# Two transformer blocks on one core: the last gate stage and the final norm with tokens on the rows

## The chip, the core and the metric

The kernel runs on one core of a Trainium2 chip. The core has five engines that work side by side, each through its own instructions in order: TensorE (PE, matrix products), VectorE (DVE), ScalarE (ACT), GpSimd (POOL) and SyncE (SP), which here only starts transfers. What one engine needs of another it waits for at a semaphore. The metric is the time of one execution on the device in microseconds (us), the median of several runs.

## The reference, cut to what matters

The whole program is two blocks of a transformer over 256 tokens of 1024 features, in float32: a feed-forward and attention block, then a block with a convolution, a forgetting attention ("fox") and two more feed-forwards. The change touches its end:

```python
def second_block(x, p, ...):
    for i in range(2):
        ...                                   # convolution (i = 0) or fox attention (i = 1)
        hn = rmsnorm_2(h, ffn_norm[i])
        h = h + jnp.square(jax.nn.relu(hn @ ffn_w1[i])) @ ffn_w2[i]
        gate = jax.nn.sigmoid(rmsnorm_2(h, ple_norm[i]) @ ple_w_gate[i])
        h = h + gate * (p[i] @ ple_w_proj[i])
    return rmsnorm_2(h, final_norm)
```

`p[i]` is 256 tokens by 256 features, `ple_w_gate[i]` is 1024 by 1024, `ple_w_proj[i]` 256 by 1024. `rmsnorm` divides a token's features by the root of their mean square and multiplies by a gain for each feature.

## The kernel before

**Layout.** Activations lie with the features on the 128 rows (partitions) and the 256 tokens along a row: eight tiles `self.x[0..7]` of 128x256. A product `dense(name, c0, X)` (lines 252 to 254) loads a 128x128 block of weights as the stationary operand and streams the 256 tokens of one X tile through it. Precision is kept by splitting both operands in a high and a low part, so that each block takes three products (weights high by X high, weights high by X low, weights low by X high). ScalarE makes the high part of a chunk of weights (L231) and VectorE the low part (L235); a chunk is eight blocks, four chunks are held converted at a time.

**The other layout**, `v_steps` (L1014 to L1016), makes the tokens the rows: 128 tokens of X are the stationary operand and 512 columns of weights stream through it. Before the change only the values of attention are made so.

**The end of fox.** The list FOX orders work that fills TensorE between the steps of the sixteen heads. Its last entry, `e1`, is `values(1)`: eight groups of `ple_value` (p times `ple_w_proj`, each group six products of 256 columns into one bank, then a scaling by 0.5 on ScalarE, L1101). The order of TensorE is written out by hand there; behind it come the products of the output weights `wo`, which a scheduler places. A head is: scores (L1036), softmax, a transpose on TensorE (L1075), a copy out by ScalarE (L1077), and the product with the values (L1471).

**Banks.** The accumulators of TensorE are eight banks in four kinds of two: `mm`, `s`, `pt`, `at`. `bank("mm")` walks through the kinds listed for the stage in CYCLE (in the heads only `mm`, in `wo` and in the feed-forward `mm`, `at`, `s`, in the last stage `mm` and `at`). A bank is written again only after its readers are done.

**The last stage, `ple(1, ...)` and `run`.** Column sums of squares on TensorE (L376) give the norm; VectorE (L390), GpSimd (L385, the power -0.5) and two products (L400) spread it over the rows as R. Then eight groups of 24 products each: VectorE multiplies by R (L1129), ScalarE takes tanh (L1130), VectorE forms (tanh + 1) times the value (L1132) and adds it to x (L1086). ScalarE squares the new x (L365) and multiplies it by the gain of the final norm (L1592), VectorE adds up the squares (L368), and TensorE transposes the gained tile for the two halves of the tokens (L1595). After the last group come the column sums of the squares, L390, L385, four scalings of 128x512 (L1603 on VectorE, L1605 on ScalarE) and four transfers of 256 KB to the output (L1606, two from SP's queue and two from ScalarE's).

Of the kernel before, what the change touches and what calls it, by code (L numbers as in the profile page):

```python
# [16 lines left out]
P = 128  # L17
# [99 lines left out]
class Kern:  # L117
# [887 lines left out]
    def v_steps(self, name, X, half, bks):  # L1005

        nc = self.nc
        bks.extend(self.bank() for _ in range(2))
        for k in range(KD):
            wk = self.weight(name, k, half * 512, 512)  # L1010
            for t in range(2):
                s = slice(t * P, (t + 1) * P)
                xh, xl = X[k][0][:, s], X[k][1][:, s]
                nc.tensor.matmul(bks[t], xh, wk[0], start=(k == 0), stop=False)  # L1014
                nc.tensor.matmul(bks[t], xl, wk[0], start=False, stop=False)
                nc.tensor.matmul(bks[t], xh, wk[1], start=False, stop=(k == KD - 1))  # L1016
                if (k, t) != (KD - 1, 1):
                    yield

# [103 lines left out]
    def ple(self, i, X, R, pv, after):  # L1123
        nc = self.nc
        self.stage = f"ple{i}"
        for n in range(KD):
# [6 lines left out]
            self.residual(t, n, after)  # L1133

# [203 lines left out]
    def fox(self, Xk, rc, R, after):  # L1338
# [143 lines left out]
        def values(i):  # L1482
            X = [self.split(t) for t in loads]
            for n in range(KD):
                pv.append(self.ple_value(i, n, X))
# [44 lines left out]
    def run(self, out):  # L1530
# [53 lines left out]
        _, R = self.stats(st["acc"])  # L1584
        f = {"acc": None}
        self.cycle = CYCLE["end"]
        tb = [[self.bank(tag) for _ in range(2)] for tag in ("s", "pt")]

        def after(n, x):
            f["acc"] = self.square_into(f["acc"], x, n == KD - 1)  # L1590
            xg = self.t("t")
            nc.scalar.mul(xg, x, self.col("final2", n))  # L1592
            for t in range(2):
                o = tb[t][n // 4][:, (n % 4) * P : (n % 4 + 1) * P]
                nc.tensor.transpose(o, xg[:, t * P : (t + 1) * P], self.ident)  # L1595

        self.ple(1, st["X"][0], R, pv, after)
        r = self.rsqrt(self.mean_eps(self.col_sums(f["acc"], "mm"), 2, D), 2)
        for t in range(2):
            for i in range(2):  # L1600
                o = self.p([P, 512], "o", 4)
                if i:
                    nc.vector.tensor_scalar(o, tb[t][i], r[:, t : t + 1], None, op0=ALU.mult)  # L1603
                else:
                    nc.scalar.mul(o, tb[t][i], r[:, t : t + 1])  # L1605
# [131 lines left out]
```

## Time and profile before

| | us |
|---|---|
| median of 3 runs (1384.69 to 1385.52) | 1385.49 |
| the profiled execution | 1383.3 |
| its span, first to last instruction | 1381.5 |
| last gate stage, first product to start of the last (1345.63 to 1371.00) | 25.4 |
| from the start of the last product to the end of the span | 10.5 |

The profiled execution lasts 1.8 us beyond its span and is 2.2 us under the median of the runs. TensorE is busy for 98% of the span; its weight loads (PEld) overlap its products.

### The profile page before, as it was taken

To read this page: it belongs to the slowest core of one execution; us is meant where nothing else is said; L and a number is where in the kernel's file an instruction comes from. 1 tells how busy PE (TensorE), PEld (TensorE's weight loads), DVE (VectorE), ACT (ScalarE), POOL (GpSimd) and SP (SyncE) were. 2 spreads that over 40 slices of the span, in tenths; PEclk is the share of its full clock that TensorE was granted. 3 is DMA by queue.
4 is the path that set the end of the run, shared out by engine and by line. 5 is a ranking of instruction groups with operands and counts; after the bars stand their busy time and mean duration, and the time that the engine had idled before them with its cause. 6 is when DMAs were issued, how large, how long until landed. Compare 5 with 4: busy or idle time off the path is not lost.

```text
span 1381.5 us, 28847 instructions
## 1 busy us (share of the span) xinstructions
PE 1360.4 (98%) x11191; PEld 1325.2 (96%) x11191; DVE 1031.1 (75%) x2306; ACT 828.2 (60%) x1875; POOL 42.4 (3%) x89
## 2 busy tenths in 40 slices
PE   9999999999999999999999999999999999999997
PEld 8999998899988999999999999999998999999997
DVE  7777658798886778876679797765578987776555
ACT  6555445678787555555555586654457786665444
POOL 0000000000000000000000000000001310000000
PEclk9999999999999999999999999999999999999999
DMA  7555556633332645555566145555554334555550
GB/s 271 186 184 184 184 182 231 226 138 108 123 105 80 199 161 193 194 182 184 183 228 227 56 153 187 187 182 182 185 178 169 133 119 152 192 189 183 183 183 35
DMA packets 65385, 234.87 MB, mean 170 GB/s; under 512 B 7552, under 2 KB 8224, under 8 KB 65248
## 3 DMA queue, kind: packets, MB, share of 16 engines
q1 hardware_dynamic: 63792, 231.42, 48.6%
q8 instruction: 88, 1.44, 0.4%
q10 hardware_dynamic: 1296, 1.35, 0.3%
q0 software_dynamic: 160, 0.26, 0.1%
q14 instruction: 49, 0.40, 0.1%
HBM read 231.95 MB, written 1.05 MB: 169 GB/s over the span
## 4 chain that ended last, share of the span: by engine, by line
PE 93%; issue 2%; DVE 2%; ACT 1%; DMA 1%; SPq 0%; POOLq 0%; DVEq 0%; POOL 0%; ACTq 0%
PE mm L252 12%; PE mm L253 12%; PE mm L254 12%; PE at L252 8%; PE at L253 8%; PE at L254 8%; PE s L252 7%; PE s L254 7%; PE s L253 7%; PE pt L1190 3%; PE pt L1075 1%; PE s L1036 1%; PE at L819 1%; DVE lo L235 1%; PE pt L376 1%
## 5 line engine op out<-in xcount | busy, mean ns | idle before, releaser
L231 ACT ACTIVATE hi<-raw 128x512 fp32r<-128x512 f32 (+1 forms) x760 | 473.5, 666 | 410.8 <-issue 227.1
L235 DVE TENSOR_TENSOR lo<-raw,hi 128x512 fp32r<-128x512 f32 (+1 forms) x760 | 537.5, 742 | 166.2 <-ACT hi L231 164.2
L252 PE MATMUL mm<-a,hi 128*128 128x256 f32 x1046 | 304.6, 291 | 1.4 <-ACT hi L231 1.4
L253 PE MATMUL mm<-a,hi 128*128 128x256 f32 x1046 | 296.2, 283 | 0.0
L254 PE MATMUL mm<-a,lo 128*128 128x256 f32 x1046 | 295.8, 283 | 0.0
L252 PEld LDWEIGHTS mm<-a,hi 128*128 128x128 f32 x1046 | 200.4, 192 | 4.5 <-issue 2.3
L253 PEld LDWEIGHTS mm<-a,hi 128*128 128x128 f32 x1046 | 200.2, 191 | 0.0
L254 PEld LDWEIGHTS mm<-a,lo 128*128 128x128 f32 x1046 | 199.9, 191 | 0.2 <-DVE lo L235 0.2
L252 PE MATMUL at<-a,hi 128*128 128x256 f32 x622 | 177.4, 286 | 1.8 <-ACT hi L231 1.6
L254 PE MATMUL at<-a,lo 128*128 128x256 f32 x622 | 177.2, 285 | 0.2 <-DVE lo L235 0.2
L253 PE MATMUL at<-a,hi 128*128 128x256 f32 x622 | 177.3, 285 | 0.0
L252 PE MATMUL s<-a,hi 128*128 128x256 f32 x516 | 147.1, 285 | 1.0 <-ACT a L1272 1.0
L254 PE MATMUL s<-a,lo 128*128 128x256 f32 x516 | 146.8, 285 | 0.2 <-DVE lo L235 0.2
L253 PE MATMUL s<-a,hi 128*128 128x256 f32 x516 | 146.7, 284 | 0.0
L252 PEld LDWEIGHTS at<-a,hi 128*128 128x128 f32 x622 | 118.8, 191 | 2.7 <-ACT hi L231 1.8
L254 PEld LDWEIGHTS at<-a,lo 128*128 128x128 f32 x622 | 119.2, 192 | 1.4 <-DVE lo L235 0.4
L253 PEld LDWEIGHTS at<-a,hi 128*128 128x128 f32 x622 | 118.9, 191 | 0.7 <-DVE a L346 0.5
L252 PEld LDWEIGHTS s<-a,hi 128*128 128x128 f32 x516 | 99.5, 193 | 1.3 <-ACT a L1272 1.2
L254 PEld LDWEIGHTS s<-a,lo 128*128 128x128 f32 x516 | 99.4, 193 | 0.4 <-DVE lo L235 0.4
L253 PEld LDWEIGHTS s<-a,hi 128*128 128x128 f32 x516 | 99.5, 193 | 0.0
L253 PE MATMUL at<-H,hi 128*128 128x256 f32 x324 | 91.7, 283 | 0.0
L252 PE MATMUL at<-H,hi 128*128 128x256 f32 x324 | 91.7, 283 | 0.0
(411 smaller groups left out, 2795.9 us busy)
## 6 DMA issues: line engine op xcount, KB each, us to landing
raw<-in_wts SPq DMA_DIRECT2D x424, 512.0 KB, 3.4
cw<-in_dwp SPq DMA_DIRECT2D x9, 704.0 KB, 4.5
x<-in_xT SPq DMA_DIRECT2D x4, 256.0 KB, 5.6
raw<-in_wts SPq DMA_DIRECT2D x2, 256.0 KB, 3.7
e<-in_pT ACTq DMA_DIRECT2D x4, 128.0 KB, 4.2
out_dram<-o ACTq DMA_DIRECT2D x2, 256.0 KB, 3.0
out_dram<-o SPq DMA_DIRECT2D x2, 256.0 KB, 3.1
cst<-in_cst SPq DMA_DIRECT2D x1, 416.0 KB, 8.1
```

Source lines behind the costliest of these rows:

```text
L231: nc.scalar.activation(hi[:, s], raw[:, s], AF.Copy)
L235: nc.vector.tensor_tensor(lo[:, s], raw[:, s], hi[:, s].bitcast(F32), op=ALU.subtract)
L252: nc.tensor.matmul(out, sh, mh, start=(first and i == 0), stop=False)
L253: nc.tensor.matmul(out, sh, ml, start=False, stop=False)
L254: nc.tensor.matmul(out, sl, mh, start=False, stop=(last and i == n - 1))
L376: self.ins = self.nc.tensor.matmul(b[:, t : t + 1], p[:, t * P : (t + 1) * P], self.ones[:, 0:1], start=(i == 0), stop=(i == len(parts) - 1),)
L819: nc.tensor.matmul(o[e * HD : (e + 1) * HD, kt * P :], V[:, kt, 2 * i + g], pt[i][:, k], start=False, stop=(i == 1 and kt == 1),)
L1036: nc.tensor.matmul(o, q[:, t * P : n], k[:, :n], start=(t == 1 and i == 0), stop=False)
L1075: nc.tensor.transpose(tb[:, o * P : (o + 1) * P], a, self.ident)
L1190: nc.tensor.matmul(o, w[:, d], x[:, g, 16 - d : 16 + P - d], start=(d == 0), stop=(d == LAGS - 1))
```

## The change

The last gate stage and the values that it needs are made with the tokens on the rows, so that the output needs no transpose after the last product.

- `values(1)` goes through `v_steps`, now for any number of X tiles: two halves of 512 columns, each of two tiles of X and two halves of the tokens, 12 products of 512 columns for a half, into two banks at once; each bank is then scaled in two pieces of 128x256 (L1575 in the new file).
- The new function `last_ple` takes the place of `ple(1, ...)`. The gains of the final norm are fetched once, the same row for all 128 partitions (a transfer on ScalarE's queue). The old x is transposed by 16 products (L1158) as soon as it is there and added to the value (L1163). The first half of the columns is made for both halves of the tokens; the second half first for tokens 0 to 127, 512 columns wide, then for tokens 128 to 255 in two pieces of 256 columns.
- `quarter`: tanh out of the bank with the norm as a scale for each row (L1170), times the value (L1171), added to x (L1173), squared with the sum along the row given out by ScalarE itself (L1175), times the gain (L1182; not for the last quarter).
- `store(t)`: norm from the four sums (L1186, L385), scaling of four quarters, shared by VectorE and ScalarE (L1189, L1190, L1193, L1194, L1196), and two transfers of 256 KB. `store(0)` stands between the products of the two halves of the tokens.
- Gone: the products that spread R (L400, two instructions), the products with R on VectorE, the final column sums on TensorE (four instructions), the gain on ScalarE.

```diff
+    def rows3(self, o, x, t, w, first, last):
+        nc = self.nc
+        s = slice(t * P, (t + 1) * P)
+        xh, xl = x[0][:, s], x[1][:, s]
+        nc.tensor.matmul(o, xh, w[0], start=first, stop=False)
+        nc.tensor.matmul(o, xl, w[0], start=False, stop=False)
+        nc.tensor.matmul(o, xh, w[1], start=False, stop=last)
...
+    def last_ple(self, X, acc, pv, out):
...
+        nc.scalar.dma_start(gains, bass.AP(tensor=src.tensor, offset=src.offset, ap=[[0, P], [1, D]]))
+        rh = self.w([P, 2], "r1", 1)
+        nc.vector.tensor_scalar(rh, self.rsqrt(self.mean_eps(self.col_sums(acc), 2, D), 2), 0.5, None, op0=ALU.mult)
...
+                for n in range(4):
+                    nc.tensor.transpose(
+                        tb[:, n * P : (n + 1) * P], self.x[4 * half + n][:, t * P : (t + 1) * P], self.ident
+                    )
...
+        def quarter(t, q, o):
+            g = self.t("u")
+            nc.scalar.activation(g, o, AF.Tanh, scale=rh[:, t : t + 1])
+            nc.vector.tensor_tensor(g, g, pv[4 * t + q], op=ALU.mult)
+            v = x[t][q // 2][:, q % 2 * T : q % 2 * T + T]
+            nc.vector.tensor_tensor(v, v, g, op=ALU.add)
+            sq = self.t("sq")
+            nc.scalar.activation(sq, v, AF.Square, accum_out=ss[:, t, q : q + 1])
...
+            if q < 3:
+                nc.vector.tensor_tensor(v, v, gains[:, q * T : (q + 1) * T], op=ALU.mult)
+        def store(t):
+            v = self.w([P, 1], "rs_1", 2)
+            nc.vector.tensor_scalar(v, ss[:, t, 3:4], 1.0 / D, pre[:, t : t + 1], op0=ALU.mult, op1=ALU.add)
+            r = self.rsqrt(v, 1)
+            a, b = x[t]
+            nc.vector.scalar_tensor_tensor(b[:, T:], b[:, T:], r, gains[:, 3 * T :], op0=ALU.mult, op1=ALU.mult)
+            nc.scalar.mul(b[:, :T], b[:, :T], r)
+            nc.sync.dma_start(out[t * P : (t + 1) * P, 512:], b)
+            if t:
+                nc.vector.tensor_scalar(a[:, :T], a[:, :T], r, None, op0=ALU.mult)
+                nc.scalar.mul(a[:, T:], a[:, T:], r)
+            else:
+                nc.scalar.mul(a, a, r)
+            nc.scalar.dma_start(out[t * P : (t + 1) * P, :512], a)
...
             X = [self.split(t) for t in loads]
-            for n in range(KD):
-                pv.append(self.ple_value(i, n, X))
+            pv.extend([None] * KD)
+            for half in range(2):
+                yield from self.v_steps(f"pp_{i}", X, half, bks := [])
+                for t in range(2):
+                    for j in range(2):
+                        v = pv[4 * t + 2 * half + j] = self.a()
+                        nc.scalar.mul(v, bks[t][:, j * T : (j + 1) * T], 0.5)
                 yield
```

A scheduler orders the instructions, so the change moves some that the diff does not name. On TensorE at the end of fox (`pt`: transpose of the last head, `at_...<-PTh`: its product with the values, `y`: the heads' results that `wo` takes; `mm`, `s`, `at_...<-y`: products of three column groups of `wo`), before:

```order
L254 MATMUL s_15805<-y_15708,lo_15809 128x256
L1075 MATMUL pt_15736<-cst,P_15683 128x128 x3
L1471 MATMUL at_15742<-PTh_15716,VS_14224 64x256
L1471 MATMUL at_15742<-PTh_15740,VS_14224 64x256
L1471 MATMUL at_15742<-PTh_15716,VS_14224 64x128
L1471 MATMUL at_15742<-PTh_15740,VS_14224 64x128
L252 MATMUL mm_15691<-y_15747,hi_15694 128x256
```

and with the change (L1081 and L1555 are the lines 1075 and 1471 of before):

```order
L1081 MATMUL pt_15708<-cst,P_15655 128x128 x3
L1555 MATMUL at_15714<-PTh_15688,VS_14224 64x256
L252 MATMUL at_15777<-y_14926,hi_15780 128x256
...
L254 MATMUL at_15777<-y_15680,lo_15781 128x256
L1555 MATMUL at_15714<-PTh_15712,VS_14224 64x256
L1555 MATMUL at_15714<-PTh_15688,VS_14224 64x128
L1555 MATMUL at_15714<-PTh_15712,VS_14224 64x128
L253 MATMUL s_15819<-y_15681,hi_15822 128x256
L254 MATMUL s_15819<-y_15680,lo_15823 128x256
L252 MATMUL mm_15663<-y_15719,hi_15666 128x256
```

The walk through the kinds of banks now stands elsewhere when `wo` begins, its third group lies in `at` instead of waiting for `mm`, and 21 products of it stand between the first and the second product of the last head, two more behind its last.

On TensorE early in the last stage, before (`mm_18578` and `at_18532`: the first two groups, `pt_18510`: the column sums):

```order
L254 MATMUL mm_18578<-a_17944,lo_18582 128x256
L252 MATMUL mm_18578<-a_18084,hi_18581 128x256
L376 MATMUL pt_18510<-ones,sq_18508 128x1
L376 MATMUL pt_18510<-ones,acc_17529 128x1
L376 MATMUL pt_18510<-ones,sq_18508 128x1
L253 MATMUL mm_18578<-a_18085,hi_18581 128x256
L253 MATMUL at_18532<-a_18505,hi_18535 128x256
```

and with the change (`pt_18485` holds the column sums, `pt_18520` and `s_18513` transposed old x):

```order
L1022 MATMUL mm_18530<-hi_18553,a_17776 128x512
L1023 MATMUL mm_18530<-hi_18553,a_17777 128x512
L1158 MATMUL s_18513<-cst,a_18474 128x128
L1024 MATMUL mm_18530<-lo_18554,a_17776 128x512
...
L376 MATMUL pt_18485<-ones,sq_18480 128x1
L376 MATMUL pt_18485<-ones,acc_17501 128x1
L376 MATMUL pt_18485<-ones,sq_18480 128x1
L1158 MATMUL pt_18520<-cst,a_18054 128x128
```

Eleven of the transposes stand ahead of the first product, one among them and the last four right behind the column sums; these four write the bank that held the sums, since `pt` has two banks.

On ScalarE at the end, before (`u`: tanh, `sq`: squares, `t`: gain, `o`: scaled output) and with the change (`at_18754`: the last product group, `o_18497` and `o_18498`: rows of tokens 128 to 255):

```order
L1130 ACTIVATE u_18893<-u_18893 128x256
L365 ACTIVATE sq_18900<-a_18898 128x256
L1592 ACTIVATE t_18902<-a_18898,cols 128x256
L1605 ACTIVATE o_18915<-s_18528,rs_y_18913 128x512
L1605 ACTIVATE o_18921<-pt_18530,rs_y_18913 128x512
L1606 DMA out_dram<-o_18915 128x512
L1606 DMA out_dram<-o_18921 128x512
```

```order
L1170 ACTIVATE u_18779<-at_18754,r_18484 128x256
L1190 ACTIVATE o_18496<-o_18496,rs_y_18713 128x256
L1196 ACTIVATE o_18495<-o_18495,rs_y_18713 128x512
L1175 ACTIVATE sq_18783,ss_18527<-o_18498 128x256
L1197 DMA out_dram<-o_18495 128x512
L1190 ACTIVATE o_18498<-o_18498,rs_y_18787 128x256
L1194 ACTIVATE o_18497<-o_18497,rs_y_18787 128x256
L1197 DMA out_dram<-o_18497 128x512
```

The scalings of the first half of the tokens (L1190, L1196) stand between the last tanh and the last square.

## Rows read from the trace of the kernel before

**Rows 1.** The head of the page.

```profile
span 1381.5 us, 28847 instructions
```

**Rows 2.** Busy time in the last stage: PE, PEld, DVE, ACT, POOL, clock, DMA, GB/s.

```profile
1345.65:1371.30 25.65, 25.65 (x219) 25.65 (x218) 18.17 (x44) 14.21 (x33) 0.69 (x1) 1.00 0.06 22
```

**Rows 3.** Timeline, TensorE's end: start, length, engine, line, names, count, [idle before].

```profile
1371.00 0.28 PE L254 MATMUL mm<-a,lo 128*128 128x256 f32 x1
...
1373.67 0.38 PE L376 MATMUL at<-ones,sq 128*128 128x1 f32 x2 [2.05 <-ACT sq L365]
```

**Rows 4.** Timeline of the other engines behind the last product.

```profile
1371.32 0.42 DVE L1129 TENSOR_TENSOR u<-mm,R 128x256 f32<-128x256 f32 x1 [0.54 <-PE mm L254]
...
1371.78 0.42 ACT L1130 ACTIVATE u<-u 128x256 f32<-128x256 f32 x1 [1.06 <-DVE u L1129]
...
1372.68 0.42 DVE L1086 TENSOR_TENSOR a<-th,a 128x256 f32<-128x256 f32 x1
1373.20 0.42 ACT L365 ACTIVATE sq<-a 128x256 f32<-128x256 f32 x1 [1.01 <-DVE a L1086]
...
1374.54 0.16 DVE L390 TENSOR_SCALAR rs_v<-at 128x2 f32<-128x2 f32 x1 [1.43 <-PE at L376]
1374.78 0.69 POOL L385 TENSOR_TENSOR rs_y<-rs_v,mhalf 128x2 f32<-128x2 f32 x1 [23.18 <-DVE rs_v L390]
1375.50 0.69 ACT L1605 ACTIVATE o<-s,rs_y 128x512 f32<-128x512 f32 x1 [1.48 <-POOL rs_y L385]
...
1376.28 1.00 SPq L1606 DMA_DIRECT2D out_dram<-o  x2
```

**Rows 5.** The output transfers by their tile.

```profile
DMA to landing us min/median/max: 2.7/3.1/3.4
```

**Rows 6.** Timeline, TensorE: 512-column products (12 steps apart), 256-column (8 apart).

```profile
262.18 0.39 PE L1015 MATMUL at<-hi,a 128*128 128x512 f32 x1
...
264.90 0.39 PE L1015 MATMUL at<-hi,a 128*128 128x512 f32 x1
...
1369.10 0.28 PE L252 MATMUL mm<-a,hi 128*128 128x256 f32 x1
...
1370.06 0.28 PE L254 MATMUL mm<-a,lo 128*128 128x256 f32 x1
```

**Rows 7.** Timeline, last stage: the products that spread R, a pair of transposes, L390.

```profile
1350.66 0.16 DVE L390 TENSOR_SCALAR rs_v<-pt 128x2 f32<-128x2 f32 x1 [2.49 <-PE pt L376]
...
1354.16 0.28 PE L254 MATMUL at<-a,lo 128*128 128x256 f32 x1
1354.29 0.61 PE L400 MATMUL pt<-diag,ones 128*128 128x128 f32 x4
...
1354.85 0.28 PE L253 MATMUL at<-a,hi 128*128 128x256 f32 x1
...
1362.65 0.27 PE L1595 MATMUL s<-cst,t 128*128 128x128 f32 x1
1362.76 0.27 PE L1595 MATMUL pt<-cst,t 128*128 128x128 f32 x1
```

**Rows 8.** Timeline, TensorE: values product of an earlier head, and the end of fox.

```profile
1128.55 0.87 PE L1471 MATMUL at<-PTh,VS 128*64 128x256 f32 x8
...
1139.94 1.51 PE L1471 MATMUL at<-PTh,VS 128*64 128x256 f32 x8
1141.92 0.38 PE L252 MATMUL mm<-y,hi 128*128 128x256 f32 x1 [0.47 <-ACT y L342]
...
1142.38 0.39 PE L253 MATMUL mm<-y,hi 128*128 128x256 f32 x1
```

**Rows 9.** Timeline, ScalarE in the last heads: scalings of values, exponential, its sum, a chunk.

```profile
1125.25 0.66 ACT L1101 ACTIVATE a<-mm 128x256 f32<-128x256 f32 x2
...
1126.31 0.47 ACT L1060 ACTIVATE P<-s,smx 128x256 f32<-128x256 f32 x1
1126.68 0.19 ACT L1060 ACTIVATION_READ_ACCUMULATOR P<-s,smx 128x1 f32 x1
...
1127.87 1.15 ACT L231 ACTIVATE hi<-raw 128x512 fp32r<-128x512 f32 x2 [0.37 <-ACT a L1101]
```

More of the change, by code (lines that the diff above doesn't have):

```diff
@@ L1008, in v_steps @@
         bks.extend(self.bank() for _ in range(2))
-        for k in range(KD):
+        n = len(X)
+        for k in range(n):
             wk = self.weight(name, k, half * 512, 512)
             for t in range(2):
[L1012 to L1017, printed above, removed]
-                    yield
+                self.rows3(bks[t], X[k], t, wk, k == 0, k == n - 1)
+                if (k, t) != (n - 1, 1):
+                    yield
+    def rows3(self, o, x, t, w, first, last):
[5 more added lines that the diff above has]
+        nc.tensor.matmul(o, xh, w[1], start=False, stop=last)
     def bc(self, v, axis, n):
@@ L1483, in values @@
             X = [self.split(t) for t in loads]
-            for n in range(KD):
-                pv.append(self.ple_value(i, n, X))
+            pv.extend([None] * KD)
+            for half in range(2):
+                yield from self.v_steps(f"pp_{i}", X, half, bks := [])
+                for t in range(2):
+                    for j in range(2):
+                        v = pv[4 * t + 2 * half + j] = self.a()
+                        nc.scalar.mul(v, bks[t][:, j * T : (j + 1) * T], 0.5)
                 yield
@@ L1583, in run @@
         self.ffn(1, st2["X"][0], R, nxt)
[L1584 to L1605, printed above, removed]
-                (nc.sync if i else nc.scalar).dma_start(out[t * P : (t + 1) * P, i * 512 : (i + 1) * 512], o)
+        self.last_ple(st["X"][0], st["acc"], pv, out)
         self.ph.close()
@@ L1674, in lay_out @@
         "bf": g["b_f_2"].reshape(1, 16),
+        "final2": g["final_norm_2"].reshape(1, D),
     }
```

35 lines of the change are left out of this document (added).

## Prediction

> **What bounds the kernel now.** I read the windows of the last stage first, then the timeline of its end, engine by engine, then the end of fox, where the order moves too. [...] The rest of the kernel, some 1100 us ahead of the end of fox, keeps its instructions and their order.
>
> **Values in the last heads.** 48 products of 256 columns become 24 of 512. Twelve steps of 512 columns take 264.90 - 262.18 = 2.72 us, 0.227 each; eight of 256 take 0.96, 0.120 each [rows 6]. A wide product saves 0.240 - 0.227 = 0.013 us, so 24 save 0.3. The eight scalings stay eight (0.66 for two [rows 9]), but a bank is now given back only after two of them, and both `mm` banks are taken at once. TensorE has about 1.3 us of scores and other products between the last write of a bank and the next first one; in that time ScalarE must do two scalings behind what is queued ahead of them. The order puts an exponential pair or a conversion there. I follow the timeline and find both just in time, and book 0.2 of loss; the bounds are 0 and, for one handover, a conversion 1.15, the exponential with its sum 0.47 + 0.19 and two scalings 0.66 [rows 9], 2.5 us, less the 1.3 of cover.
>
> **The end of fox.** Three holes are seen there. The last head's product with the values takes 1.51 us where an earlier one takes 0.87, so 0.64 in it is a wait for ScalarE's copy; then 0.47 until the head's result is there; then the low part: two steps take 1142.38 - 1141.92 = 0.46, some 0.12 over what they need [rows 8]. With the change 21 products of `wo` (2.5 us) stand in the first hole, two (0.24) in the second, and more groups stand ready in the third. They are needed anyway, so the gain is 0.64 + 0.24 + 0.12 = 1.0, less 0.1 for each of two switches of the kind of product: **0.8**, bounds 0 and 1.2. Nothing is removed here; the walk through the banks only lets the third group of `wo` start early.
>
> **The fetch of the gains.** It stands on ScalarE's queue behind the conversion of a chunk and lies in memory that fox has used, so it waits for the last product of `wo`. Queued behind it are the high parts of the last three x tiles, for which the next feed-forward waits. An issue holds a queue for half of 1.00 us [rows 4]. TensorE has 45 products of three groups that need none of those tiles, 45 x 0.120 = 5.4 us; the three splits need about 2.5 after the fetch. I cost it at nothing; without that cover it would cost the 0.5.
>
> **The last stage on TensorE.** Out: spreading R, 1354.85 - 1354.16 = 0.69 us for what are two steps of 0.120 without it, 0.45 [rows 7]. Shorter: 72 products of 512 columns for 144 of 256, 72 x 0.013 = 0.96; the last 48 stay at 256. Added: sixteen transposes before the last product, where fourteen stood; one costs 1362.76 - 1362.65 = 0.11 [rows 7], so 0.22, and 0.1 for each of three places where they are put in, 0.3. Added too is a wait: the last four transposes write the bank that held the column sums, so they wait for L390. Before, VectorE stood idle 2.49 us for those sums [rows 7]; now a half chunk, four sums and another chunk are queued ahead of L390 on it, and by my count they end about when the sums do. What is left is L390's 0.16 [rows 7] and the way there and back, 0.3 together; the bounds are 0.2 and 1.3 (VectorE still at a whole chunk). Behind the waiting transposes stand all products of the stage. Sum: 0.45 + 0.96 - 0.22 - 0.3 - 0.3 = **0.6** gained, bounds -0.4 and 0.9.
>
> [...]
>
> The supply of weights is near. In the second half the first 128 tokens use up a chunk in six products, 1.4 us, and a conversion on ScalarE alone takes 1.15 [rows 9]. Four chunks are held: the last is free when the first half ends, and wanted 18 products, 4.1 us, later. In between stand two tanh of 0.42 [rows 4], 1.15 on ScalarE and about 0.7 more on VectorE, under 3 us. It is covered by a microsecond; each one beyond costs itself.
>
> **The tail**, counted from the start of the last product. Before: product with R at 0.32, tanh 0.78, x at 1.68, square 2.20, the sums' L390 at 3.54, the power 3.78, first scaling 4.50; the second issue on SP's queue begins near 5.9 (1376.28 and half of 1.00 [rows 3, 4]). With the change: tanh reads the bank at 0.32; the product with the value at 0.9 (0.46 later as in [rows 4], and VectorE may still scale the first tokens); the sum with x at 1.35; the square 0.52 behind its start as in [rows 4], at 1.87. On ScalarE two scalings of the first 128 tokens stand between tanh and square, 0.4 and 0.69 [rows 4], over at about 1.7: just in time. The square's sum is out 0.37 + 0.19 later [rows 9], at 2.43. The norm's L1186 starts at 2.5, the power 0.24 on at 2.74, the scalings 0.72 on at 3.46; two follow each other on either engine, 0.9 together, and the last issue begins at 4.4. That is 1.5 earlier. The issues of the first tokens are out at 1.1 and 2.4, so two transfers end together instead of four; landing took 2.7 to 3.4 [rows 5], and I take 0.3 of the difference, between 0 and 0.7. Tail: **1.8**, bounds 1.0 (the square waits for the scalings, no help at landing) and 2.3.
>
> **The sum** against the profiled execution: 0.3 - 0.2 + 0.8 + 0.6 + 1.8 = 3.3 us; I take 3.2, a tenth left for order elsewhere. Its span of 1381.5 becomes 1378.3 [rows 1], the execution 1383.3 becomes 1380.1. That execution is 2.2 under the median of the runs, 1385.49, so the forecast for the median is 1385.5 - 3.2 = **1382.3**. A measurement of this kernel can tell some 0.2%, 2.8 us, from no change.
>
> **The rivals.**
> - The end of fox gives nothing. For it: the last heads are near the limit of ScalarE too, and if the softmax of the last two heads runs later by what TensorE is earlier, its holes only move. Against it: the 21 products stand in the hole whatever comes before. It gives 3.2 - 0.8 - 0.3 for a handover = 2.1 gained, 1383.4: no change that can be told. Chance 0.21.
> - Wide products cost as much as two narrow ones (the spacing then follows from columns alone): 1.28 less gain, and 0.1 of handover back, 2.0 gained, 1383.5. [...] Against it: [rows 6]. Chance 0.06.
> - The tail gains only 0.8, since the chain still crosses four engines and the square comes behind the first tokens' scalings: 2.2 gained, 1383.3. Chance 0.11.
> - Slower: the handover of banks in the last heads. If ScalarE gets to the two scalings behind a conversion and an exponential each time, TensorE waits 2.5 - 1.3 = 1.2 us at each of three handovers, scores and softmax of the next head start later by that, and what ScalarE has lost comes back at the next head: with the wait and its echo 2.4 for each, 7.2, less the forecast's other gains and with nothing at the end of fox, 3.2 - 0.8 - 0.1 = 2.3: 4.9 slower, 1390.4. It decides from the point where the queue ahead of the scalings ends more than 1.3 us after the bank's last product. Against it: ScalarE has 0.37 idle there [rows 9]. Chance 0.05.
>
> **How the numbers follow.** The forecast has 0.57 and is faster by over 0.2%; the three small gains have 0.38 and are within it; slower has 0.05. The best of all bounds is 0.3 + 1.2 + 0.9 + 2.3 = 4.7, 1380.8; the worst without the slower rival is -0.1 + 0 - 0.4 + 1.0, 0.5 gained, 1385.0. From 1380.7 to 1384.7 leaves out the slower rival, the corner of the bounds and little else, under 0.2.
>
> **What would show it.** In the new profile: steps of 0.227 in the last stage; the waits of TensorE there one of 0.3 for L390 and no other; from the last product's start to the end of the span 8.7 us instead of 10.5; at the end of fox one hole under 0.3. Wrong would be the forecast if TensorE waits in the heads for L1575, if a wait for a chunk stands in the last stage's second half, or if the last issue begins later than 5 us after the last product.

## The result

Before: 1385.09 us (median of four runs). With the change: 1376.47 us (four runs, 1375.6 to 1377.9). The ratio is 0.9939 with an interval from 0.9925 to 0.9953: faster by 8.6 us (6.5 to 10.4 by the interval), where 3.2 had been forecast with a range that ended at 1380.7. The direction was right and the size was not. The time lies outside the range, so the question is where the other 5 us came from. One mechanism that no part of the forecast names holds most of them.

The profiled execution of the changed kernel has a span of 1373.8 us, 7.7 less than [rows 1]. I went through the two traces with marks that both have, and asked at each how far the one is ahead of the other:

| stretch | before, us | after, us | gain, us | forecast |
|---|---|---|---|---|
| start of the span to the 61st product | 16.00 | 15.21 | 0.8 | 0 |
| four stretches of products with H, together | 310.56 | 307.12 | 3.4 | 0 |
| last product with H to start of the last product | 25.63 | 24.72 | 0.9 | 0.6 |
| start of the last product to the end | 10.53 | 7.65 | 2.9 | 1.8 |
| all the rest, values and end of fox among it | 1018.80 | 1019.09 | -0.3 | 0.9 |

The first line is no effect of the change: in the eighteen traces of this study the 61st product starts anywhere between 14.7 and 16.9 us, and TensorE's order up to there is the same in all.

The second line is the surprise. H are the tiles that the second matrix of a feed-forward takes as its moving operand. Nothing there was edited, and the order on the engines is the same. The timeline of TensorE at the first and the last of the 768 products of the last feed-forward, start and length first, before:

```profile
1253.33 0.28 PE L252 MATMUL at<-H,hi 128*128 128x256 f32 x1
...
1345.37 0.28 PE L254 MATMUL s<-H,lo 128*128 128x256 f32 x1
```

and with the change:

```profile
1250.41 0.28 PE L252 MATMUL mm<-H,hi 128*128 128x256 f32 x1
...
1341.43 0.28 PE L254 MATMUL at<-H,lo 128*128 128x256 f32 x1
```

The reader is to divide (a step is the time from the start of one product to the start of the next): 92.04 us over 767 steps is 120.0 ns a step, 91.02 us is 118.7. TensorE is busy throughout in both, 92.04 of 92.04 us and 91.02 of 91.02 at a granted clock of 1.00, and waits for nothing, so no view that shows waits or busy shares can show this; only the distance between products does. The two stages with 768 such products gain 1.02 us each, the two with 528 gain 0.70 each.

What did change there is an address. The change has three small tiles more in a pool that lives for the whole kernel (four sums of squares for both halves of the tokens, a partial sum, the final norm), 128 bytes per partition, and everything that is allocated behind that pool moved up by 128 bytes: H began at byte 32 of each 256, as the weights do, and begins at byte 160 now. Below, distance stands for how far the moving operand begins behind the weights, modulo 256 bytes: for H it was 0 and is 128.

The last stage on TensorE, as busy time by windows (PE, PEld, DVE, ACT, POOL, clock, DMA, GB/s), to be set beside [rows 2], and its timeline: a run of 512-column products six steps apart, the transposes behind the column sums, L390, and the last product:

```profile
1341.56:1366.43 24.87, 24.87 (x146) 21.70 (x144) 18.25 (x49) 12.24 (x33) 1.24 (x2) 1.00 0.07 22
```

```profile
1348.23 0.36 PE L376 MATMUL pt<-ones,sq 128*128 128x1 f32 x2
1348.45 0.63 PE L1158 MATMUL pt<-cst,a 128*128 128x128 f32 x4
1348.84 0.48 PE L1022 MATMUL mm<-hi,a 128*128 128x512 f32 x1
...
1353.72 0.39 PE L1022 MATMUL at<-hi,a 128*128 128x512 f32 x1
...
1355.08 0.39 PE L1022 MATMUL at<-hi,a 128*128 128x512 f32 x1
...
1366.15 0.28 PE L1024 MATMUL at<-lo,a 128*128 128x256 f32 x1
```

```profile
1348.63 0.16 DVE L390 TENSOR_SCALAR rs_v<-pt 128x2 f32<-128x2 f32 x1 [0.28 <-PE pt L376]
```

TensorE is busy for the whole of the stage, 24.87 of 24.87 us, as it was before [rows 2], so its length hangs on the number and the spacing of its products. Six wide steps take 1.36 us, 0.227 each, as forecast. The four transposes start at 1348.45, ahead of L390 at 1348.63: they don't wait for it.

Behind the last product the length of a chain counts; before, TensorE sat idle in it for 2.05 us [rows 3]. The other engines there, to be set beside [rows 4]:

```profile
1366.47 0.47 ACT L1170 ACTIVATE u<-at,r 128x256 f32<-128x256 f32 x1 [0.55 <-PE at L1024]
1366.84 0.50 ACT L1190 ACTIVATE o<-o,rs_y 128x256 f32<-128x256 f32 x1
1367.24 0.71 ACT L1196 ACTIVATE o<-o,rs_y 128x512 f32<-128x512 f32 x1
1367.95 0.42 ACT L1175 ACTIVATE sq<-o 128x256 f32<-128x256 f32 x1
...
1369.44 0.51 ACT L1190 ACTIVATE o<-o,rs_y 128x256 f32<-128x256 f32 x1 [0.98 <-POOL rs_y L385]
...
1370.38 0.35 ACTq L1197 DMA_DIRECT2D out_dram<-o  x1
```

```profile
1366.98 0.43 DVE L1171 TENSOR_TENSOR u<-u,a 128x256 f32<-128x256 f32 x1
1367.44 0.42 DVE L1173 TENSOR_TENSOR o<-o,u 128x256 f32<-128x256 f32 x1
1368.50 0.21 DVE L1186 TENSOR_SCALAR rs<-ss,pre 128x1 f32<-128x1 f32 x1 [0.64 <-ACT sq L1175]
```

```profile
DMA to landing us min/median/max: 2.0/2.1/2.3
```

Counted from 1366.15 the chain reads: tanh 0.32, product 0.83, sum 1.29, square 1.80, L1186 2.35, scaling 3.29, last issue 4.23. Forecast were 0.32, 0.9, 1.35, 1.87, 2.5, 3.46 and 4.4. The landing (last row) is 0.7 to 1.1 us shorter than [rows 5].

### The profile page after: what moved, and what is told of

Same layout as the page of the kernel before. It is cut to its first block, busy times and chain, and to the rows that moved or that the text cites. A ratio compares the mean times of both kernels' runs of the same rounds, so it can differ in the third digit from the quotient of the medians.

```text
span 1373.8 us, 28642 instructions
## 1 busy us (share of the span) xinstructions
PE 1354.7 (99%) x11083; PEld 1314.2 (96%) x11083; DVE 1029.5 (75%) x2310; ACT 824.7 (60%) x1877; POOL 43.0 (3%) x90
## 4 chain that ended last, share of the span: by engine, by line
PE 94%; DVE 2%; ACT 1%; DMA 1%; issue 0%; SPq 0%; POOL 0%; POOLq 0%; DVEq 0%; ACTq 0%
PE mm L252 12%; PE mm L253 12%; PE mm L254 12%; PE at L253 8%; PE at L252 8%; PE at L254 8%; PE s L252 7%; PE s L254 7%; PE s L253 6%; PE pt L1274 3%; PE pt L1081 1%; PE s L1042 1%; PE mm L1022 1%; PE mm L1024 1%; PE mm L1023 1%; PE at L819 1%
## 5 line engine op out<-in xcount | busy, mean ns | idle before, releaser
L252 PE MATMUL mm<-a,hi 128*128 128x256 f32 x990 | 288.2, 291 | 1.2 <-ACT hi L231 1.2
L253 PE MATMUL mm<-a,hi 128*128 128x256 f32 x990 | 280.1, 283 | 0.0
L254 PE MATMUL mm<-a,lo 128*128 128x256 f32 x990 | 279.9, 283 | 0.0
L252 PEld LDWEIGHTS mm<-a,hi 128*128 128x128 f32 x990 | 189.6, 192 | 4.0 <-issue 2.3
L253 PEld LDWEIGHTS mm<-a,hi 128*128 128x128 f32 x990 | 189.5, 191 | 0.0
L254 PEld LDWEIGHTS mm<-a,lo 128*128 128x128 f32 x990 | 189.2, 191 | 0.2 <-DVE lo L235 0.2
L252 PE MATMUL at<-a,hi 128*128 128x256 f32 x598 | 170.1, 285 | 1.2 <-ACT hi L231 1.0
L253 PE MATMUL at<-a,hi 128*128 128x256 f32 x598 | 170.3, 285 | 0.1
L254 PE MATMUL at<-a,lo 128*128 128x256 f32 x598 | 170.1, 285 | 0.3 <-DVE lo L235 0.2
L252 PEld LDWEIGHTS at<-a,hi 128*128 128x128 f32 x598 | 114.0, 191 | 2.2 <-ACT hi L231 1.3
L254 PEld LDWEIGHTS at<-a,lo 128*128 128x128 f32 x598 | 114.4, 191 | 1.5 <-DVE lo L235 0.7
L253 PEld LDWEIGHTS at<-a,hi 128*128 128x128 f32 x598 | 114.2, 191 | 0.8 <-DVE a L346 0.6
L252 PE MATMUL mm<-H,hi 128*128 128x256 f32 x324 | 91.2, 281 | 0.0
L254 PE MATMUL at<-H,lo 128*128 128x256 f32 x324 | 91.2, 281 | 0.0
```

The costliest lines, as they stand in the source:

```text
L252: nc.tensor.matmul(out, sh, mh, start=(first and i == 0), stop=False)
L253: nc.tensor.matmul(out, sh, ml, start=False, stop=False)
L254: nc.tensor.matmul(out, sl, mh, start=False, stop=(last and i == n - 1))
```

## Experiments

**Is it the address?** Two runs take the 128 bytes apart from the code. The first gives them to the kernel before:

```diff
+        nc.gpsimd.memset(self.w([P, 32], "pad", 1), 0.0)
         _, R = self.stats(st2["acc"])
         nxt, st = self.normed(["ple1"])
```

> The kernel before with one tile of 128 bytes more per partition, placed where the change puts its three small tiles; no instruction but one memset of it on GpSimd is added, the order on the engines stays. Theory (placement): the tiles of the stages move by 128 bytes, and the 2592 products that read H go from 120.0 to 118.7 ns apart as in the profile of the changed kernel; 2592 x 0.00134 = 3.5 us faster, about 1381.6. Rival (the code, or this chip's run, makes those stretches quicker): 120.0 ns stays and the time is that of before, 1385 within 1 us.

The second takes them from the changed kernel:

```diff
-        ss = self.w([P, 2, 4], "ss8", 1)
-        pre = self.w([P, 2], "pre", 1)
+        ss = self.p([P, 2, 4], "ss8", 1)
+        pre = self.p([P, 2], "pre", 1)
...
-            v = self.w([P, 1], "rs_1", 2)
+            v = self.p([P, 1], "rs_1", 2)
```

> The changed kernel with its three small tiles taken out of the work pool and put behind the last stage's own tiles, so that H, y and the tiles of the heads lie where they lay before; the order on every engine is that of the changed kernel. Theory (placement): the products with H are 120.0 ns apart again and 3.5 us of the 8.6 go, about 1380; what is left against before, some 5 us, is the gain of the code itself. Rival: 1376.5 within 1 us.

Measured: 1380.33 and 1380.39 us beside 1384.15, ratios 0.9974 (0.9965 to 0.9984) and 0.9972 (0.9962 to 0.9982). Empty bytes alone make the old kernel 3.8 us faster, and the new kernel without them has 3.8 us left. In the first, the 768 products with H take 91.03 us; in the second, 92.04 again:

```profile
1251.31 0.28 PE L252 MATMUL at<-H,hi 128*128 128x256 f32 x1
...
1342.34 0.28 PE L254 MATMUL s<-H,lo 128*128 128x256 f32 x1
```

```profile
1252.83 0.28 PE L252 MATMUL mm<-H,hi 128*128 128x256 f32 x1
...
1344.87 0.28 PE L254 MATMUL at<-H,lo 128*128 128x256 f32 x1
```

So the place is shown as a cause, and the code's own gain is 3.8 us, 2.5 to 5.3 by the interval.

**Which part of the code?** The same kernel with the values made as before, so that the end of fox has its old order too:

```diff
-            pv.extend([None] * KD)
-            for half in range(2):
-                yield from self.v_steps(f"pp_{i}", X, half, bks := [])
...
+            for n in range(KD):
+                pv.append(self.ple_value(i, n, X))
                 yield
```

> The changed kernel, its small tiles behind the last stage's own as in the run before, with the values made as before (feature-major, 48 products of 256 columns), so that the end of fox has the order of before; only the last stage and the norm are new. The values are then added to the wrong elements, which costs no time. Theory (all of the code's gain is in the last stage and behind it): last stage 24.7 us and 7.6 us from its last product's start to the end as in the changed kernel, and 3.8 us faster than before in all. Rival (forecast): values and end of fox hold 0.9 of the gain, so only about 2.9 us faster, and the stretch from the last scores to the last feed-forward's H products is as long as before while that of the changed kernel is shorter.

Measured: 1380.02 beside 1384.08, ratio 0.9969 (0.9956 to 0.9981), 4.1 us; 24.7 us for the last stage and 7.65 behind it. The theory holds: without values and end of fox nothing is lost. By the time alone the rival's 2.9 us would still fit, since its ratio of 0.9979 lies in the interval; the trace decides. From the last scores to the first product with H it takes 120.37 us, as in the kernel before, and the changed kernel without the 128 bytes has 120.30, so the end of fox holds 0.07 of its 0.8. The end of fox alone was tried in the kernel before:

```diff
         self.stage = "wo"
         self.cycle = CYCLE["wo"]
+        self.turn += 1
```

> The kernel before with the walk through the banks moved on by one at the start of wo, so that 21 products of wo stand between the first and the second pair of products of the last head with its values, as in the changed kernel; nothing else. Forecast's term (the hole goes and the wo products were needed anyway): 0.8 us less from the last scores of the last head to the first product with H of the last feed-forward, 120.4 us before, so 119.6. Theory now (each further change between the two kinds of product, and each walk from bank to bank, costs about 0.1, and the split product pays again what the hole held): 120.2 to 120.4.

From the last scores to the first product with H it takes 120.79 us (1134.07 to 1254.86) beside the 120.37 of the kernel before. Both numbers miss: it isn't 0.8 shorter, nor the same, but 0.4 longer. TensorE's timeline there shows of what:

```profile
1135.93 0.52 PE L1075 MATMUL pt<-cst,P 128*128 128x128 f32 x3 [0.25 <-DVE P L1459]
...
1138.84 0.65 PE L1471 MATMUL at<-PTh,VS 128*64 128x256 f32 x2
1139.42 0.39 PE L252 MATMUL at<-y,hi 128*128 128x256 f32 x1
...
1142.12 0.86 PE L1471 MATMUL at<-PTh,VS 128*64 128x256 f32 x6
1143.45 0.39 PE L252 MATMUL mm<-y,hi 128*128 128x256 f32 x1 [0.47 <-ACT y L342]
```

The first line is a wait of 0.25 for VectorE's softmax result, ahead of the last head's product; neither the kernel before nor the changed one waits there. The rest is the split. From the start of the last head's product to the first product of `wo` behind it the kernel before takes 1141.92 - 1139.94 = 1.98 us [rows 8], and this run 1143.45 - 1138.84 = 4.61, of which 21 products of `wo` in between, at 0.117 each, are 2.46. That leaves 2.15, 0.17 more than the group in one piece with its hole. So filling the 0.64 that I read as a wait wins nothing: a second beginning and end of the group, with one more change of kind on either side, cost as much and 0.17 more. The hole of 0.47 stands as before. In the changed kernel more groups of `wo` are ready for that one, and it shrinks to some 0.2, which pays for the split and no more.

**The tail.** To see what the early transfers are worth I first moved their call behind the last product.

```diff
         for j in range(2):
             quarter(0, 2 + j, o[:, j * T : (j + 1) * T])
-        store(0)
...
             quarter(1, 2 + j, o)
+        store(0)
         store(1)
```

> The changed kernel, its small tiles behind the last stage's own, with the norm, scalings and transfers of the first 128 tokens put behind the last product instead of between the two halves' products. Theory (two transfers in flight at the end land sooner than four): from the last issue to the end 4.6 us as before the change instead of 3.4, the last issue about 1 us later for four more scalings, 9.5 to 10 us from the last product's start to the end instead of 7.6. Rival (the landing of the last transfers doesn't depend on the others): from the last issue to the end 3.4 us, 8.6 us in all.

That told nothing: 7.65 us from the last product's start to the end, with every issue where it was; the scheduler had put the work back in the same place. What the program's text says of order is not the order. A dependence says it: one norm for both halves of the tokens, with the call again behind the last product.

```diff
         def store(t):
-            v = self.p([P, 1], "rs_1", 2)
-            nc.vector.tensor_scalar(v, ss[:, t, 3:4], 1.0 / D, pre[:, t : t + 1], op0=ALU.mult, op1=ALU.add)
-            r = self.rsqrt(v, 1)
+            if t == 0:
+                v = self.p([P, 2], "rs_1", 1)
+                nc.vector.tensor_scalar(v, ss[:, :, 3], 1.0 / D, EPS, op0=ALU.mult, op1=ALU.add)
+                nc.vector.tensor_tensor(v, v, pre, op=ALU.add)
+                self.r12 = self.rsqrt(v, 2)
+            r = self.r12[:, t : t + 1]
```

> The changed kernel, its small tiles behind the last stage's own, with one norm for both halves of the tokens behind the last square, so that the scalings and transfers of the first 128 tokens can't come ahead of the last product (in the run before this one the order on the engines had stayed as it was). Theory (two transfers in flight at the end land sooner than four): from the last issue to the end 4.6 us instead of 3.4, the last issue 1 us later for the further scalings, 9.7 us from the last product's start to the end instead of 7.65. Rival (landing doesn't depend on the other transfers): 3.4 us behind the last issue, 8.6 in all.

The last issue and the landing in its trace:

```profile
1375.42 0.35 ACTq L1200 DMA_DIRECT2D out_dram<-o  x1
```

```profile
DMA to landing us min/median/max: 2.1/2.4/2.8
```

The last product starts at 1369.82, the last issue at +5.60, the end is at +9.48: 1.83 lost, 1.37 of it in the issue and 0.46 behind it. From the last issue to the end it takes 3.88 us, between the two expectations. The three kernels stand in the order in which their four issues are spread: within 0.72 us before, 4.59 to the end; within 1.31 here, 3.88; within 3.0 with the change, 3.42. That fits the theory, but it is an order of three kernels and no proof of the cause.

**What in the place does it?** H in the two feed-forwards of the second block, at mixed distances, first each tile for itself and then high and low part together:

```diff
-            H.append(self.split(h, 1.0, self.p([P, T], "H", 2 * KF2, F32R), self.p([P, T], "H", 2 * KF2, F32R)))
+            H.append(self.split(h, 1.0, self.p([P, T + 8], "H", 2 * KF2, F32R)[:, :T], self.p([P, T + 8], "H", 2 * KF2, F32R)[:, :T]))
```

> The kernel before with the tiles H of the two feed-forwards of the second block 1056 bytes apart instead of 1024, so that the 64 of them lie at every multiple of 32 modulo 1024; instructions and order stay. Theory (placement): the spacing of the products follows from where the moving operand begins: 120 ns at 32 modulo 256, 118.7 at 160 modulo 256, about 117 where it begins at a multiple of 64 (as the tiles y at 192 modulo 512 show), so half of the 1536 products gain 3 ns and some of the others 1.3, some 2.7 us in all. Rival: one spacing for all of them.

```diff
-            H.append(self.split(h, 1.0, self.p([P, T], "H", 2 * KF2, F32R), self.p([P, T], "H", 2 * KF2, F32R)))
+            hl = self.p([P, 2 * T + 8], "H", KF2, F32R)
+            H.append(self.split(h, 1.0, hl[:, :T], hl[:, T : 2 * T]))
```

> The kernel before with high and low part of each H of the two feed-forwards of the second block in one tile, 2080 bytes from one to the next, so that both parts begin at the same residue modulo 256 and the 32 pairs go through all eight multiples of 32; instructions and order stay. Theory (the moving operand's place relative to the weights', which begin at 32 modulo 256, sets the spacing): triples of products with H are 120.0 ns a product at residue 32 and there alone, 118.7 at 160, and 116 to 118 at the others; the kernel is about 3 us faster. Rival (what counted was that high and low part lay apart, or which tile was which): no such order by residue.

Both gained as expected (1380.68 and 1380.27, one run each; the 768 products take 90.35 and 90.13 us), and in the second the triples with tiles at distance 96 were the quickest, 115.3 ns a product; those at distance 0 took 117.0, where its theory had 120.0. I believed that table, and it misled, as the runs after these show: the time of a triple among changing distances isn't that of a steady distance.

Weights and operands moved together, by a first constant tile that is 32 bytes longer:

```diff
-        self.cols = self.cp.tile([P, COLW], F32, name="cols")
+        self.cols = self.cp.tile([P, COLW + 8], F32, name="cols")[:, :COLW]
```

> The kernel before with the first constant tile 32 bytes longer, so that everything behind it begins 32 bytes later: the tiles a, H and the chunks now begin at 64 modulo 128 instead of 32; instructions and order stay. Theory (placement): if a product of 256 columns is 117 instead of 120 ns apart when its moving operand begins at a multiple of 64, some 9400 products with a, H and y gain about 3 ns each, 27 us: about 1358. Rival (only some particular tiles matter, or where they lie to one another): less than 4 us either way.

1384.28 beside 1384.15 (0.9994 to 1.0012), and 120.0 ns still for the products with `a` and H. Here an address that is a multiple of 64 gained nothing; the rival holds, that it is how the tiles lie to one another. Only the products with `y` in fox, at distance 160 in both kernels, went from 117.3 to 118.7 ns, a first sign that the distance isn't the whole of it.

This trace shows something else, too. From the last product's start to the end it has 11.13 us instead of 10.53. Windows of its idle time behind the last products and of the column sums after it, then the column sums in the kernel before:

```profile
1371.40:1374.00 2.60, 0.61 (x7) 0.52 (x5) 1.27 (x3) 0.82 (x3) 0.00 (x0) 1.00 0.00 0
1374.10:1375.60 1.50, 1.50 (x7) 1.50 (x8) 0.06 (x1) 0.31 (x1) 0.00 (x0) 0.50 0.00 0
```

```profile
1373.70:1375.00 1.30, 1.08 (x8) 0.84 (x8) 0.16 (x1) 0.32 (x1) 0.22 (x1) 1.00 0.00 0
```

TensorE had been idle for 2.06 us here and 2.05 there; here its granted clock fell from 1.00 to 0.50 before the last sums, and there it did not. It fell so in two of the ten traces with the old end. The new end has no product behind that hole and can't lose these 0.6 us.

So I moved the operands alone, by a gap between the weights and the tiles `a` and all that follows:

```diff
+        self.gap = pool("gap", 1)
         self.actp = pool("act", NA)
...
+        nc.gpsimd.memset(self.gap.tile([P, 24], F32, name="gap"), 0.0)
```

> The kernel before with 96 bytes left empty between the chunks of weights and the tiles a, so that a and H begin at 128 modulo 256 while the weights stay at 32; instructions and order stay, but for one memset of the empty bytes on GpSimd. Theory (what counts is where the moving operand begins relative to the weights, modulo 256; 96 is the quickest of the eight distances, 115.3 ns against 120.0 at distance 0): 6552 products with a and 2592 with H gain up to 4.7 ns each, 43 us, about 1342; less where the conversions or the transfers become the limit. Rival (the products with a are held by something else): only the 2592 with H gain, 12 us, about 1372. Against both: moving weights and operands together changed nothing.

> The changed kernel, its small tiles behind the last stage's own, with the same 96 bytes between the weights and the tiles a. Theory: the gain of the code, 3.8 us, and that of the place, 6312 products with a and 2592 with H at up to 4.7 ns, 42 us, add up: about 1339, faster than both kernels of this case. Rival: the place gives 12 us, about 1368, or the gain of the code goes into new waits for conversions.

Both expectations fell: 1386.88 beside 1384.19 (ratio 1.0019, 1.0010 to 1.0028) and 1382.57 (0.9988, 0.9979 to 0.9997). At a steady distance of 96 the products with `a` and H are 120.0 ns apart. The wide products went from 227 to 234 ns (medians), which cost the changed kernel 0.3 us of its last stage (25.03). The trace of the first is the other one with the lower clock at the end, 11.13 us there again. A steady table was needed: a gap ahead of each feed-forward's own tiles, another in each stage.

```diff
         self.pp = self.ph.enter_context(self.tc.tile_pool(name=name, bufs=2, reuse_waits="pool"))
+        gap = {'w2': 32, 'f2w2': 64, 'ffn0': 160, 'ffn1': 192}.get(name)
+        if gap:
+            self.nc.gpsimd.memset(self.p([P, gap // 4], "gap", 1), 0.0)
```

> The kernel before with an empty tile ahead of the stage's own tiles in the four feed-forward stages: 32, 64, 160 and 192 bytes, so that all H of a stage begin at one distance from the weights: 32, 64, 160 and 192 modulo 256. Order stays. Seen so far with one distance throughout: 120.0 ns a product at distance 0 (H, a, in five kernels) and 96 (H, a), 118.7 at 128 (H), 117 at 160 (y). Theory A (the steady distance modulo 256 sets it, as such a table): 117 in the third stage, and one value each for the other three that differs from 120 in some. Theory B (the distances that were quick were quick because neighbouring tiles began at different residues): 120.0 in all four.

> As the run before, with 224, 128, 32 and 64 bytes in the four stages. Theory A: 118.7 in the second stage as in the changed kernel, and in the third and fourth stage the values that the first and second stage of the run before show, since the distance alone counts, not the stage. Theory B: 120.0 in the first, third and fourth.

These two took 1373.74 and 1378.72 us beside 1383.18, one run each. Measured, as length of a stretch over its steps (527 in the first two stages, 767 in the others): distance 32, 117.8 in both of its stages; 64, 117.8 in both; 128, 118.7; 160, 117.3; 224, 118.3; 192, 113.4; 0 and 96, 120.0. Theory A held in these two runs, and in every stretch the products keep one repeating pattern throughout. The quickest, at 192, from the first of the two:

```profile
1248.84 0.29 PE L255 MATMUL at<-H,hi 128*128 128x256 f32 x1
...
1335.79 0.28 PE L257 MATMUL s<-H,lo 128*128 128x256 f32 x1
```

These are 86.95 us where there were 92.04. With `a` and H both moved, in the kernel before and in the changed one (the gap of above with 32 or 192 bytes):

> The kernel before with 32 bytes left empty between the weights and the tiles a: a and H at distance 32. Theory A: products with a and with H take the same spacing, the one that the first stage of the run with 32 bytes shows (117 by the y tiles at this distance: some 25 us faster, about 1358). Rival: the products with a stay at 120.0 whatever the distance, since the tile that they read was written by another way, and the time stays within 3 us of 1384.

> The same with 32 bytes: a and H at distance 32, where the kernel before became 24.5 us faster with 116.7 ns for both. Theory: the same 3.3 ns for 8904 products, 29 us, of which the kernel before kept 24.5; so about 1356. Rival: the code's gain of 3.8 us doesn't add up with it, since the last stage's 512-column products then read their stationary tiles a at another distance (233 instead of 227 ns at 96): some 0.7 us less.

> The changed kernel, its small tiles behind the last stage's own, with 192 bytes left empty between the weights and the tiles a: a and H at distance 192, at which the H of one stage were 113.4 ns apart in the run with four gaps. Theory A (the distance alone sets it): 6312 products with a and 2592 with H at 113.4 instead of 120.0, 59 us less than the 1380.4 of the same kernel without the gap: about 1322, where supply and waits give some of it back. Rival (what else is read and written beside them matters as much: at distance 32 the H were 117.8 where only they had moved and 116.7 where a had moved too): anything from 113 to 120, a gain of less than 59 but still some.

The old kernel with 32 empty bytes takes 1358.65 us, beside 1383.18, one run each: 24.5 less, from 116.7 ns for products with H and nearly all with `a`. That is not the 117.8 that theory A had for this distance, so the distance alone doesn't set it. The changed kernel with 32 bytes takes 1355.27 (ratio 0.9789, 0.9774 to 0.9804) and with 192 bytes 1353.09 (0.9774, 0.9747 to 0.9801): both beat both kernels of this case, by some 20 us and more, and place and code add up. With 192 the single runs go from 1346.2 to 1359.4, and the one trace shows what may differ from run to run, in the first and the second stretch of products with H, 528 each:

```profile
132.38 0.28 PE L253 MATMUL mm<-H,hi 128*128 128x256 f32 x1
...
192.11 0.28 PE L255 MATMUL at<-H,lo 128*128 128x256 f32 x1
...
618.55 0.28 PE L253 MATMUL mm<-H,hi 128*128 128x256 f32 x1
...
680.62 0.28 PE L255 MATMUL at<-H,lo 128*128 128x256 f32 x1
```

59.73 us and 62.07, 113.3 and 117.8 ns a product, at the same distance. In the last stage H and weights even begin at the same bytes as in the first run with four gaps: 113.4 there, 117.8 here. So theory A falls, as the whole of it: one distance showed more than one rhythm. What decides between them, and what the engine does in the 6.7 ns between the quickest and the slowest, stays open.

## Why the forecast was wrong, point by point

- **The step that failed** is the sentence that the rest of the kernel "keeps its instructions and their order", read as if time followed from those. Order and instructions did stay; 2592 products among them became 1.3 ns shorter, since three tiles of a few bytes moved the operands. That is 3.4 us by the trace, and the same 128 bytes in the kernel before give 3.8 us by its run times. It is the largest part of the miss, and nothing in the sum or among the rivals stood for it. Without it the time would have come out near 1380.3, still just below the range's end of 1380.7; the tail and the scatter of the runs hold the rest.
- **Values**, forecast 0.1: nothing, within 0.1. Counted from the 61st product, the changed kernel without the 128 bytes is 0.39 ahead at the end of the third stretch of products with H, 100 us before the values, and 0.31 at the last scores behind them. The wait for the scaling of a bank that the forecast booked at 0.2 is in the changed kernel's trace at one handover:

```profile
1124.99 0.50 PE L1022 MATMUL mm<-hi,a 128*128 128x512 f32 x1 [0.22 <-ACT a L1575]
```

- **End of fox**, forecast 0.8 (bounds 0 and 1.2): 0.07, close to the lower bound. The mis-sized terms are the 0.64, which filling the hole did not win, and the switches, booked at 0.1 each by the author's estimate, which no row gave: the run with the end of fox alone paid 0.17 more than the hole. The rival that gave this part nothing was right about the place. Its reason, that the softmax comes later, shows in that run as 0.25 of wait, but not in the changed kernel.
- **Last stage**, forecast 0.6: 0.9. The spacing came as booked, the 0.3 for L390 did not, and the sum without it is the 0.9 measured; spreading of R and transposes, with the estimate of 0.1 for each of their three places, weren't measured by themselves. Here the forecast and the text before it misread the names: the last four transposes write the bank of the first four of that kind, whose readers are long done, not that of the column sums. They begin before L390 reads those, and a bank is written again only after its readers are done (the wait of 0.22 above). The 512-column products came 227 ns apart, as in [rows 6], beside two of 120 in the same stage, so the rival of wide products without a saving fails there. For 256 columns the quickest rhythm of the runs is 113.3 ns and the slowest 120.0, so the 120 of [rows 6] was one rhythm of several, not a price.
- **Tail**, forecast 1.8 (bounds 1.0 and 2.3): 2.9, above the bound. The chain was right within 0.2 at every step: 1.7 by the last issue where 1.5 was forecast (before, that issue began at 5.94 in the trace; the forecast's own rows give 5.8, not its 5.9). Behind the last issue 1.2 us were saved where 0.3 was booked and 0.7 was the bound. The later experiment gives 0.46 of it back when the transfers come closer together again; the other 0.7 isn't taken apart.
- **Fetch of the gains**: no wait for it is seen, as booked at nothing. **Supply of weights** in the second half: the last 512-column products run at 227 ns without a wait, as forecast. **Slower by handovers**: refuted; the one wait for L1575 is 0.22.

So the code's gain was forecast at 3.2 and is 3.8 by the runs and 3.8 in the last stage and tail by the trace, with a different split than forecast: two terms too high by 0.9, two too low by 1.4. That the sums lie so close is in part luck. The rest of the 8.6 is place, 3.8 by the run with the empty bytes, and some 1.0 of scatter: the kernel before has 1385.09 us here, and 1384.1 to 1384.3 beside the later experiments with nine runs of it and more.

## What to carry to other kernels

Compare the spacing of unedited products in a new trace before you credit an edit with the time: a few bytes more in a long-lived pool move every tile behind it, and 24.5 of 1383.18 us hung on that in this kernel, whose TensorE is busy for 98% of the span. To time an edit by itself, put its new tiles behind everything else, or give the old kernel the same empty bytes. A hole inside a group of products is only worth filling if splitting the group doesn't cost the same again; here it cost 0.17 us more than the hole.

## What the runs showed of the hardware

- In these runs the spacing of back-to-back products of 128x256, at a granted clock of 1.00, differed with the distance, as counted above, from the weights to the moving operand: 120.0 ns at a steady distance of 0 in every trace that has it and at 96 (the two runs with a gap of 96 bytes), and 113.3 to 118.7 at the others tried. Moving both together, by a first constant tile 32 bytes longer, left the products with `a` and H at 120.0.
- The spacing kept one repeating pattern through stretches of 527 or 767 steps, with means of 113.3, 116.7, 117.3, 117.8, 118.3, 118.7 or 120.0 ns, and in the run with 192 bytes one distance showed 113.3 in one stage and 117.8 in three others of one execution. TensorE counts as busy at 120.0 and at 118.7 alike, 92.04 of 92.04 us and 91.02 of 91.02.
- For 128x512 products the medians were 227 ns at distance 0 and 234 with the stationary tiles moved by 96 bytes, while the products of 256 columns took 120.0 at both.
- After a hole of some 2 us TensorE's granted clock fell from 1.00 to 0.50 in some executions and not in others: at the end in two of the ten traces with the old end, the hole being 2.06 us in one of them and 2.05 in the kernel before, where it stayed 1.00. All eighteen traces have a wait of 2.0 to 2.6 us for the softmax between 1060 and 1085 us; in five of them the clock is 0.50 for a while behind it. In the kernel with the old values, one of the five, the way from the third to the fourth stretch of products with H takes 248.33 us, beside 246.96 before. Its hole, and a window of the products behind it:

```profile
1083.77 0.55 PE L1081 MATMUL pt<-cst,P 128*128 128x128 f32 x3 [2.06 <-DVE P L1543]
```

```profile
1085.00:1087.00 2.00, 2.00 (x11) 2.00 (x11) 1.57 (x6) 1.24 (x4) 0.07 (x1) 0.50 0.05 6
```
